# A hybrid decoder layer: block sums of the MLP weights tied to the order of ScalarE and GpSimd, a quarter of them formed in SBUF, output stores on GpSimd's queue

## The chip, the cores and the metric

One core of a Trainium2 chip runs the whole layer in one launch. The time is device microseconds (us) of the execution. Engines are TensorE (PE), VectorE (DVE), ScalarE (ACT), GpSimd (POOL) and SyncE (SP). DMAs are issued from the queues of SP, ScalarE and GpSimd, and all of them are carried out by the core's 16 DMA engines. Each engine takes its instructions in the order in which they stand.

## The reference

All in float32, 2048 tokens of width 1024, one layer:

```
h = rms_norm(x, norm1_g)
z = h @ w_in                         # 1024 x 2052, cut among four mixers: SGU (uv), S5, RG-LRU (cx, gate), attention (q, k, v, f)
y = concat(sgu(..), s5(..), rglru(..), forgetting_attention(..))
x = x + group_rms_norm(y) @ w_out
h = rms_norm(x, norm2_g)
x = x + square(relu(h @ w_mlp_in)) @ w_mlp_out      # 1024 x 4096, 4096 x 1024
return rms_norm(x, final_g)
```

## The kernel before

The layer runs in three stretches. `z_phase` multiplies the normed tokens by `w_in`, and between the matmuls emits the SGU, the RG-LRU and the set-up and scan of S5. `Att.run` does the attention, with the output projection (`wout_jobs`) filled in between; the rest of the projection follows, and stores the rows of `x1`, the input of the MLP, from GpSimd's queue (line 1369). `MLP.run` does the last two matrix products and the final norm.

Each float32 operand is split into two rounded parts: `split` makes the high part on ScalarE (line 54) and the low part on VectorE (line 58), and three matmuls stand for one product.

The MLP multiplies blocks with seven products in place of eight: tables `FIRST` and `SECOND` say for product `i` which one or two weight blocks, and which one or two token blocks, are added or subtracted first, and to which results the product goes. The tokens are worked in two halves of 1024, the 4096 inner columns in two weight halves `c`. For each pair of half and `c` there are seven groups of first products in `IN_ORDER` (1, 4, 5, 7, 3, 2, 6), and seven groups of second products in `OUT_ORDER` (3, 5, 6, 1, 2, 4, 7); a group is one `i` and 8 steps `p`, and a step is 12 matmuls. That makes 56 groups, of 96 matmuls each. Weights are made `AHEAD` = 2 steps before use.

Where product `i` needs the sum of two weight blocks, the sum is formed in DRAM ahead of time by `weight_sums`, for all such `i` but 1: a job copies 512 KB of the first block to a DRAM tile (`S1` or `S2`, line 1423, on SP's queue), and two jobs later a DMA on GpSimd's queue adds the second block to it (line 1426). There are 64 jobs: 32 for `S1` (`w_mlp_in`) and 32 for `S2` (`w_mlp_out`). `first_weight` and `second_weight` then load the finished sum with one DMA into one of five buffers of the pool `m_rw` (`weight`, line 1511). For `i` = 1 the two blocks are loaded with two DMAs into a buffer of the pool `m_raw` (line 1495), also five, which the blocks of the tokens share, and GpSimd forms the difference (`united`, line 1488).

TensorE's order is written by hand. On the other engines a scheduler places the instructions by its own estimates, within their dependences. `Clock` counts the matmul time written so far, and calls the next job of `weight_sums` at 90 and then every 8 of its units (`SUMS`). The copies wait for nothing, so that call sets no place for them on SP. What is left of the jobs after attention is written at once. The helper `behind(tc, engine)` keeps what is written inside it behind the last instruction written for that engine.

The results of the MLP are gathered in eight tiles `acc` of 128 x 1024. They are loaded from `x1` at the first step of a half (line 1654), and `finish` norms each and stores it (line 1600), both on SP's queue. The tiles of the second half are those of the first, so each load waits for the store of its tile.

Of the kernel before, what the change touches and what calls it, by code (L numbers as in the profile page):

```python
# [5 lines left out]
F32 = mybir.dt.float32  # L6
# [8 lines left out]
ADD, SUB, MUL, MAX = ALU.add, ALU.subtract, ALU.mult, ALU.max  # L15
EPS = 1e-6
SP, ACT, DVE, POOL = (getattr(mybir.EngineType, n) for n in ("SP", "Activation", "DVE", "Pool"))
# [25 lines left out]
def behind(tc, eng):  # L43

    ins = next(i for i in reversed(tc.nc.cur_bb.bb.instructions) if i.engine == eng)
    return tc.issue_after(ins)
# [1349 lines left out]
IN_ORDER = (1, 4, 5, 7, 3, 2, 6)  # L1396
OUT_ORDER = (3, 5, 6, 1, 2, 4, 7)
AHEAD = 2


def weight_sums(nc, w1, w2, S1, S2):


    jobs = []
    for c in range(2):
        def second(x):
            return w2[(c * 2 + x[0]) * 1024:(c * 2 + x[0] + 1) * 1024, x[1] * 512:(x[1] + 1) * 512]

        def first(x):
            return w1[x[1] * 512:(x[1] + 1) * 512, (c * 2 + x[0]) * 1024:(c * 2 + x[0] + 1) * 1024]  # L1410

        for S, side, table, n, at in ((S1, 0, FIRST, 128, first), (S2, 1, SECOND, 256, second)):
            for i in IN_ORDER:
                if (i, c) in S:
                    a, b, _ = table[i][side]
                    for r in range(4):
                        rs = slice(r * n, (r + 1) * n)
                        jobs.append((S[i, c][rs], at(a)[rs], at(b)[rs]))
    LAG = 2
    for n in range(len(jobs) + LAG):  # L1420
        if n < len(jobs):
            to, a, _ = jobs[n]
            nc.sync.dma_start(out=to, in_=a)
        if n >= LAG:
            to, _, b = jobs[n - LAG]
            nc.gpsimd.dma_start(out=to, in_=b, accum_op=ADD)
        yield


class MLP:  # L1430
# [80 lines left out]
        self.nc.sync.dma_start(out=flat(raw, block), in_=block)  # L1511
        return self.parts(raw)

    def weight_difference(self, blocks):
        return self.parts(self.united(self.load(blocks), -1))

    def parts(self, raw):
        wh = self.wp.tile([128, 512], F32R, tag="wh", name="wh")
# [7 lines left out]
    def first_weight(self, c, i, p):  # L1526

        a, b, sign = FIRST[i][0]
        rows = lambda w, f: w[:, f:f + 128].rearrange("(k p) f -> p k f", p=128)
        if (i, c) in self.S1:  # L1530
            return self.weight(rows(self.S1[i, c], p * 128))
        w = [rows(self.w1[x[1] * 512:(x[1] + 1) * 512], self.tile_row(c, p, x[0])) for x in (a, b) if x]
        return self.weight_difference(w) if b else self.weight(w[0])

    def second_weight(self, c, i, p):

        a, b, sign = SECOND[i][1]
        if (i, c) in self.S2:
            return self.weight(self.S2[i, c][p * 128:(p + 1) * 128])
        w = [self.w2[f:f + 128, x[1] * 512:(x[1] + 1) * 512] for x in (a, b) if x for f in (self.tile_row(c, p, x[0]),)]  # L1540
        return self.weight_difference(w) if b else self.weight(w[0])

    def hidden_side(self, i, p):

# [46 lines left out]
    def finish(self, half, tt, gf):  # L1591
        nc, sm, acc = self.nc, self.sm, self.acc[tt]
        ss = sm.tile([128, 1], F32, tag="fss", name="fss")
        rs = sm.tile([128, 1], F32, tag="frs", name="frs")
        jk = self.jkp.tile([128, self.D], BF16, tag="jk", name="jk")
        nc.scalar.activation(out=jk, in_=acc, func=AF.Square, accum_out=ss)
        rsqrt_(nc, sm, rs, ss, 1.0 / self.D, "fn")
        nc.vector.scalar_tensor_tensor(out=acc, in0=acc, scalar=rs, in1=gf, op0=MUL, op1=MUL)
        r0 = half * self.HT + tt * 128
        nc.sync.dma_start(out=self.out[r0:r0 + 128, :], in_=acc)  # L1600

    def run(self):
        nc, P, NP = self.nc, self.P, self.NP
# [45 lines left out]
        nxt, more, part = 1, iter(()), iter(())  # L1649
        for n, (half, c, out, i, p) in enumerate(steps):  # L1650
            if c == 0 and not out and i == IN_ORDER[0] and p == 0:
                for tt in range(self.HT // 128):
                    self.acc[tt] = accp.tile([128, self.D], F32, tag=f"acc{tt}", name="acc")
                    nc.sync.dma_start(out=self.acc[tt], in_=self.x1[half * self.HT // 128 + tt])
                k = self.halves.index(half) + 1
                more = self.prep(self.halves[k]) if k < len(self.halves) else iter(())
            if n % 2 and n > 10:
                next(more, None)
            make(n + AHEAD)
# [34 lines left out]


RATES = 2.3, 0.5
SUMS = 90.0, 8.0
NX, NO, XB = 2, 3, 2


def hybrid_kernel(tc, A, out, T=2048):
    nc = tc.nc
    with ExitStack() as top:
# [9 lines left out]
                 v=dp.tile([T, 4, 2, 64], F32, name="v"), ys=dp.tile([T, 1024], F32, name="ys"),  # L1713
                 negc=dp.tile([4, T], F32, name="negc"), x1=[dp.tile([128, 1024], F32, name=f"x1_{t}") for t in range(T // 128)],
                 hT=[[dp.tile([128, 512], F32, name=f"hT_{k}_{q}") for q in range(T // 512)] for k in range(8)])
        S1, S2 = ({(i, c): dp.tile(shape, F32, name=f"{nm}_{i}{c}") for i in IN_ORDER if table[i][side][1] and i != 1
                   for c in range(2)} for shape, table, side, nm in (([512, 1024], FIRST, 0, "s1"), ([1024, 512], SECOND, 1, "s2")))
        D5 = s5_scratch(dp)
        r8 = cp.tile([128, NPR], F32, name="r8")
        pool = lambda es, n, b, **k: es.enter_context(tc.tile_pool(name=n, bufs=b, reuse_waits="tile", **k))  # L1720
# [10 lines left out]
            cst["ii"] = ii  # L1731

        ck = Clock()
        sums = weight_sums(nc, A["w_mlp_in"][0], A["w_mlp_out"][0], S1, S2)
        ck.set_slow(sums, *SUMS)
        with tc.manual_schedule(engines={mybir.EngineType.PE}):
            side = ExitStack()
# [97 lines left out]
```

## Time and profile before

| | |
|---|---|
| median of 3 runs | 2598.64 us (2598.39 to 2600.78) |
| profiled execution | 2608.09 us, its span 2606.4 us |
| TensorE busy | 2211.0 us, 85% |
| VectorE busy | 1650.5 us, 63% |
| ScalarE busy | 1174.2 us, 45% |
| GpSimd busy | 749.5 us, 29% |
| mean granted TensorE clock | 0.921 of full |
| moved by DMA | 434.50 MB, mean 167 GB/s |

The profile is of one execution; busy time leaves out the issuing of DMAs. The granted clock is a share of full speed (1 is 2.4 GHz, 0.5 is 1.2 GHz). Times within the execution count from the start of its span. The stretches of the program lie about so: `z_phase` to 740 us, attention to 1210, the rest of the output projection to 1289, the MLP to 2591, and the last norms to the end.

### The profile page before, as it was taken

Reading aid. Unit: us, or ns where it says so; the run is one execution under the profiler, and the core shown is the slowest. Engines: PE = TensorE matmul, PEld = TensorE weight load, DVE = VectorE, ACT = ScalarE, POOL = GpSimd, SP = SyncE. Lnnn points to the kernel's source line nnn. Section 1 sums busy time; section 2 is a strip of 40 time slices with the busy share of each in tenths; the row PEclk is TensorE's granted clock in tenths of the full one; section 3 lists DMA queues with packets and bytes.
Section 4 is the critical chain, followed back from the end, with each engine's and each line's share of the span. In section 5 each row is a group of like instructions: output and inputs, shape, how many; then the busy total and the mean of one; then the engine's idle time right before and its main releaser. Section 6 shows DMA issues by size and latency. Waiting matters only on the chain.

```text
span 2606.4 us, 31889 instructions
## 1 busy us (share of the span) xinstructions
PE 2211.0 (85%) x10077; PEld 1796.1 (69%) x10077; DVE 1650.5 (63%) x3776; ACT 1174.2 (45%) x2351; POOL 749.5 (29%) x844
## 2 busy tenths in 40 slices
PE   6655247988957998978799999999997999999997
PEld 5443235776745787867577777888786887788886
DVE  6442234666634666744366698576986769757698
ACT  4210012543424564634257643576345763357543
POOL 2223334332220000101231374213722137232261
PEclk8777668999978999989899999999998999999999
DMA  7889988144245555537976543654437544365323
GB/s 179 241 212 270 258 191 169 59 112 144 76 134 171 172 169 186 154 110 252 325 213 198 176 152 102 191 174 144 126 120 257 174 153 129 100 196 181 97 86 113
DMA packets 338777, 434.50 MB, mean 167 GB/s; under 512 B 41840, under 2 KB 210832, under 8 KB 338352
## 3 DMA queue, kind: packets, MB, share of 16 engines
q1 hardware_dynamic: 301520, 352.63, 43.7%
q0 software_dynamic: 32704, 73.54, 11.6%
q10 hardware_dynamic: 4384, 6.29, 0.7%
q8 instruction: 80, 1.31, 0.2%
q14 instruction: 89, 0.73, 0.1%
HBM read 369.30 MB, written 130.12 MB: 192 GB/s over the span
## 4 chain that ended last, share of the span: by engine, by line
PE 47%; DMA 11%; DVE 6%; issue 3%; POOL 2%; ACT 2%; SPq 1%; ACTq 0%; POOLq 0%; DVEq 0%
PE pi L1564 7%; PE pi L1562 7%; PE pi L1563 7%; PE po L1587 6%; PE po L1588 6%; PE po L1589 6%; DMA q<-qk 3%; PE s L1087 2%; PE t L50 1%; PE po L1362 1%; DMA x<-x 1%; PE po L1364 1%; PE po L1363 1%; DMA ngc<-negc 1%; POOL s L1549 1%
## 5 line engine op out<-in xcount | busy, mean ns | idle before, releaser
L58 DVE TENSOR_TENSOR wl<-raw,wh 128x512 fp32r<-128x512 f32 x448 | 371.7, 835 | 55.9 <-ACT wh L54 54.0
L1562 PE MATMUL pi<-bh,wh 128*128 128x512 f32 x896 | 355.0, 396 | 36.2 <-ACT wh L54 26.0
L1587 PE MATMUL po<-wh,sh 128*128 128x512 f32 x896 | 353.0, 394 | 20.7 <-DVE acc L1578 17.6
L1549 POOL TENSOR_TENSOR s<-c 128x512 f32<-128x512 f32 x160 | 254.8, 1597 | 369.2 <-DVE sl L58 303.4
L1564 PE MATMUL pi<-bh,wl 128*128 128x512 f32 x896 | 353.3, 394 | 0.8 <-DVE wl L58 0.8
L1563 PE MATMUL pi<-bl,wh 128*128 128x512 f32 x896 | 352.8, 394 | 0.1
L1588 PE MATMUL po<-wl,sh 128*128 128x512 f32 x896 | 351.2, 392 | 0.0
L1488 POOL TENSOR_TENSOR raw<-raw 128x512 f32<-128x512 f32 x144 | 213.9, 1489 | 470.9 <-DMA raw<-hT 218.2
L1589 PE MATMUL po<-wh,sl 128*128 128x512 f32 x896 | 347.9, 391 | 0.0
L54 ACT CAST wh<-raw 128x512 fp32r<-128x512 f32 x448 | 276.4, 618 | 120.4 <-PE pi L1563 78.3
L1562 PEld LDWEIGHTS pi<-bh,wh 128*128 128x128 f32 x896 | 170.7, 191 | 75.0 <-ACT wh L54 27.2
L58 DVE TENSOR_TENSOR sl<-s,sh 128x512 fp32r<-128x512 f32 x160 | 189.1, 1190 | 43.6 <-ACT sh L54 40.7
L436 PE MATMUL z<-wh,hl 128*128 128x512 f32 (+1 forms) x384 | 160.4, 418 | 65.6 <-ACT wh L382 43.6
L1587 PEld LDWEIGHTS po<-wh,sh 128*128 128x128 f32 x896 | 169.6, 189 | 60.9 <-DVE acc L1578 20.4
L54 ACT CAST sh<-s 128x512 fp32r<-128x512 f32 x160 | 99.6, 622 | 246.2 <-PE po L1588 209.8
L1564 PEld LDWEIGHTS pi<-bh,wl 128*128 128x128 f32 x896 | 170.5, 190 | 39.5 <-DVE wl L58 3.8
L1563 PEld LDWEIGHTS pi<-bl,wh 128*128 128x128 f32 x896 | 170.8, 191 | 36.0 <-DVE bl L58 0.5
L1589 PEld LDWEIGHTS po<-wh,sl 128*128 128x128 f32 x896 | 169.5, 189 | 35.8
L1588 PEld LDWEIGHTS po<-wl,sh 128*128 128x128 f32 x896 | 169.8, 190 | 34.4
L438 PE MATMUL z<-wh,hl 128*128 128x512 f32 (+1 forms) x384 | 150.0, 391 | 6.9 <-DVE hl L58 6.9
L437 PE MATMUL z<-wl,hl 128*128 128x512 f32 (+1 forms) x384 | 150.6, 392 | 5.7 <-DVE wl L388 5.7
L1102 ACT ACTIVATE p<-p,ng 128x512 f32<-128x512 f32 (+3 forms) x160 | 103.8, 652 | 89.2 <-DVE ng L1098 89.1
(358 smaller groups left out, 4310.8 us busy)
## 6 DMA issues: line engine op xcount, KB each, us to landing
raw<-s SPq DMA_DIRECT2D x256, 256.0 KB
raw<-hT SPq DMA_DIRECT2D x192, 256.0 KB
raw<-in_w_mlp_in_dram SPq DMA_DIRECT2D x128, 256.0 KB
raw<-in_w_mlp_out_dram SPq DMA_DIRECT2D x128, 256.0 KB
x<-in_x_dram SPq DMA_DIRECT2D x32, 512.0 KB
s<-in_w_mlp_in_dram SPq DMA_DIRECT2D x32, 512.0 KB
s<-in_w_mlp_in_dram POOLq DMA_DIRECT2D x32, 512.0 KB, 14.2
s<-in_w_mlp_out_dram SPq DMA_DIRECT2D x32, 512.0 KB
```

The lines of the kernel that those rows point to most:

```text
L54: nc.scalar.copy(out=hi, in_=src)
L58: nc.vector.tensor_tensor(out=lo, in0=src, in1=hi.bitcast(F32), op=SUB)
L436: nc.tensor.matmul(pz, lhsT=hi[:, k, sl], rhs=wh, start=(k == 0), stop=False)
L437: nc.tensor.matmul(pz, lhsT=hi[:, k, sl], rhs=wl, start=False, stop=False)
L1488: self.nc.gpsimd.tensor_tensor(out=raw[:, 0], in0=raw[:, 0], in1=raw[:, 1], op=ADD if sign > 0 else SUB)
L1549: self.nc.gpsimd.tensor_tensor(out=s, in0=src, in1=self.C[b[1], b[0], p], op=ADD if sign > 0 else SUB)
L1562: nc.tensor.matmul(pt, lhsT=wh[:, sl], rhs=bh[:, k], start=(k == 0), stop=False)
L1563: nc.tensor.matmul(pt, lhsT=wh[:, sl], rhs=bl[:, k], start=False, stop=False)
L1564: nc.tensor.matmul(pt, lhsT=wl[:, sl], rhs=bh[:, k], start=False, stop=(k == 3))
L1587: nc.tensor.matmul(po[t], lhsT=sh[:, ts], rhs=vh, start=(p == 0), stop=False)
L1588: nc.tensor.matmul(po[t], lhsT=sh[:, ts], rhs=vl, start=False, stop=False)
L1589: nc.tensor.matmul(po[t], lhsT=sl[:, ts], rhs=vh, start=False, stop=(p == self.NP - 1))
```

## The change

The jobs of the sums are tied to the order of ScalarE and GpSimd where they are written: the copy is issued from ScalarE's queue behind ScalarE's last instruction, the add from GpSimd's queue behind GpSimd's last, three jobs later in place of two. `S1` is kept for `c` = 0 alone, so there are 48 jobs, called at 110 and then every 9 units. For `c` = 1 the first weights of `i` = 5, 7, 2 and 6 are loaded as two blocks, as those of `i` = 1 are, and united on GpSimd with the table's sign. `acc` tile `p` is loaded in step `p` of the fourth group (`i` = 7) of a half, behind SP's last instruction. The final stores go out from GpSimd's queue.

```diff
-def weight_sums(nc, w1, w2, S1, S2):
+def weight_sums(tc, w1, w2, S1, S2):
...
-    LAG = 2
+    LAG = 3
     for n in range(len(jobs) + LAG):
         if n < len(jobs):
             to, a, _ = jobs[n]
-            nc.sync.dma_start(out=to, in_=a)
+            with behind(tc, ACT):
+                nc.scalar.dma_start(out=to, in_=a)
         if n >= LAG:
             to, _, b = jobs[n - LAG]
-            nc.gpsimd.dma_start(out=to, in_=b, accum_op=ADD)
+            with behind(tc, POOL):
+                nc.gpsimd.dma_start(out=to, in_=b, accum_op=ADD)
         yield
...
-    def weight_difference(self, blocks):
-        return self.parts(self.united(self.load(blocks), -1))
+    def weight_pair(self, blocks, sign):
+        return self.parts(self.united(self.load(blocks), sign))
...
-        return self.weight_difference(w) if b else self.weight(w[0])
+        return self.weight_pair(w, sign) if b else self.weight(w[0])
...
-        nc.sync.dma_start(out=self.out[r0:r0 + 128, :], in_=acc)
+        nc.gpsimd.dma_start(out=self.out[r0:r0 + 128, :], in_=acc)
...
             if c == 0 and not out and i == IN_ORDER[0] and p == 0:
-                for tt in range(self.HT // 128):
-                    self.acc[tt] = accp.tile([128, self.D], F32, tag=f"acc{tt}", name="acc")
-                    nc.sync.dma_start(out=self.acc[tt], in_=self.x1[half * self.HT // 128 + tt])
                 k = self.halves.index(half) + 1
                 more = self.prep(self.halves[k]) if k < len(self.halves) else iter(())
+            if c == 0 and not out and i == IN_ORDER[3]:
+                self.acc[p] = accp.tile([128, self.D], F32, tag=f"acc{p}", name="acc")
+                with behind(self.tc, SP):
+                    nc.sync.dma_start(out=self.acc[p], in_=self.x1[half * self.HT // 128 + p])
...
-SUMS = 90.0, 8.0
+SUMS = 110.0, 9.0
...
-        S1, S2 = ({(i, c): dp.tile(shape, F32, name=f"{nm}_{i}{c}") for i in IN_ORDER if table[i][side][1] and i != 1
-                   for c in range(2)} for shape, table, side, nm in (([512, 1024], FIRST, 0, "s1"), ([1024, 512], SECOND, 1, "s2")))
+        S1 = {(i, 0): dp.tile([512, 1024], F32, name=f"s1_{i}0") for i in IN_ORDER if FIRST[i][0][1] and i != 1}
+        S2 = {(i, c): dp.tile([1024, 512], F32, name=f"s2_{i}{c}") for i in OUT_ORDER if SECOND[i][1][1] and i != 1 for c in range(2)}
```

The order in which the instructions stand, at three places. In these rows a tile `s_21` is the sum of product 2 for `c` = 1 (`S1` where it comes from `w_mlp_in`, `S2` where from `w_mlp_out`), and `raw` takes blocks of weights or tokens.

SP in `z_phase`, before: the last copies of the sums and the loads of `w_in` (line 377) that follow them.

```order
L711 DMA dT<-in_s_d_dram 16x8x1
L1423 DMA s_21_122<-in_w_mlp_in_dram 128x1024 x2
L1423 DMA s_61_124<-in_w_mlp_in_dram 128x1024 x4
L1423 DMA s_41_126<-in_w_mlp_out_dram 256x512 x4
L1423 DMA s_71_128<-in_w_mlp_out_dram 256x512 x4
L1423 DMA s_31_130<-in_w_mlp_out_dram 256x512 x4
L1423 DMA s_61_132<-in_w_mlp_out_dram 256x512 x2
L377 DMA raw<-in_w_in_dram 128x256 x6
```

The same place on SP now:

```order
L711 DMA dT<-in_s_d_dram 16x8x1
L377 DMA raw<-in_w_in_dram 128x256 x10
L377 DMA raw<-in_w_in_dram 128x2x256 x4
L377 DMA raw<-in_w_in_dram 128x260 x3
L406 DMA x<-in_x_dram 128x1024 x4
```

And ScalarE now, at its second copy of a sum, behind a store of the S5 input `zb` (line 565):

```order
L563 COPY zb<-z 128x256
L565 DMA zb<-zb 128x256
L1426 DMA s_50_117<-in_w_mlp_in_dram 128x1024
L382 ACTIVATE wh<-raw,g_172 128x256 x2
L561 ACTIVATE gg<-z 128x256
```

No copy of a sum is left on SP, and ScalarE has them one at a time between its own work; on SP the loads of `w_in` stand next to each other.

GpSimd at the end of attention, before: the last scaled outputs of the attention are stored to `ys`, then rows of `x1`.

```order
L1369 DMA x_14_83<-x 128x1024
L1166 TENSOR_SCALAR yo<-yo,rs 128x256 x4
L1167 DMA ys<-yo 128x4x256
L1369 DMA x_15_84<-x 128x1024
L1369 DMA x_1_70<-x 128x1024
L1369 DMA x_2_71<-x 128x1024
```

And now:

```order
L1369 DMA x_14_83<-x 128x1024
L1166 TENSOR_SCALAR yo<-yo,rs 128x256 x4
L1167 DMA ys<-yo 128x4x256
L1430 DMA s_31_122<-in_w_mlp_out_dram 256x512 x3
L1430 DMA s_61_124<-in_w_mlp_out_dram 256x512 x4
L1369 DMA x_15_84<-x 128x1024
L1369 DMA x_1_70<-x 128x1024
L1369 DMA x_2_71<-x 128x1024
```

Seven adds of sums have come between the store of `ys` and the next store of `x1` (an eighth stands a little ahead); each waits for its copy.

SP where the first half of the tokens ends and the second begins, before: final stores, loads of `acc`, and the two blocks of the first weights (line 1495).

```order
L1511 DMA raw<-in_w_mlp_in_dram 128x4x128 x3
L1600 DMA out_dram<-acc 128x1024
L1511 DMA raw<-in_w_mlp_in_dram 128x4x128
L1600 DMA out_dram<-acc 128x1024
L1654 DMA acc<-x_4_73 128x1024
L1495 DMA raw<-hT_0_105 128x512
L1654 DMA acc<-x_5_74 128x1024
L1600 DMA out_dram<-acc 128x1024 x2
L1495 DMA raw<-hT_0_89 128x512
L1654 DMA acc<-x_6_75 128x1024
L1654 DMA acc<-x_7_76 128x1024
L1495 DMA raw<-in_w_mlp_in_dram 128x4x128 x2
```

GpSimd at the same place now, with the stores among the adds of weight and token blocks (line 1492 is line 1488 of before):

```order
L1553 TENSOR_TENSOR s<-c 128x512 x10
L1604 DMA out_dram<-acc 128x1024 x3
L1492 TENSOR_TENSOR raw<-raw 128x512
L1604 DMA out_dram<-acc 128x1024
L1492 TENSOR_TENSOR raw<-raw 128x512 x3
L1604 DMA out_dram<-acc 128x1024 x2
L1492 TENSOR_TENSOR raw<-raw 128x512 x2
L1604 DMA out_dram<-acc 128x1024 x2
L1492 TENSOR_TENSOR raw<-raw 128x512 x13
```

The stores have left SP for GpSimd, and the loads of `acc` have left this place for the fourth group.

## Rows read from the trace of the kernel before

**Rows 1.** The page: the span in 40 slices, tenths (clock, load of DMA engines).

```profile
PEclk8777668999978999989899999999998999999999
DMA  7889988144245555537976543654437544365323
```

**Rows 2.** Windows by stage; the first line names the columns.

```profile
core 0: us, PE busy (x) PEld busy (x) DVE busy (x) ACT busy (x) POOL busy (x), PEclk, DMA share, GB/s
...
80.00:440.00 360.00, 185.57 (x682) 136.36 (x683) 138.24 (x767) 50.95 (x116) 118.27 (x172) 0.71 0.96 234
440.00:740.00 300.00, 274.07 (x1372) 221.93 (x1371) 198.54 (x424) 140.29 (x320) 97.03 (x202) 0.97 0.34 101
740.00:1200.00 460.00, 380.87 (x1999) 314.71 (x1997) 254.38 (x806) 219.47 (x573) 43.83 (x119) 0.91 0.50 158
1200.00:1289.30 89.30, 70.66 (x315) 55.14 (x314) 36.70 (x86) 27.95 (x55) 16.68 (x23) 0.90 0.91 312
```

**Rows 3.** TensorE's waits, 80 to 440 us: total us, times, longest us.

```profile
PE z L436 <- ACT wh L382: 43.6, 5, 35.6
PE z L448 <- ACT uvs L572: 43.4, 1, 43.4
```

**Rows 4.** ScalarE's waits, 80 to 440 us.

```profile
ACT wh L382 <- DMA raw<-in_w_in_dram: 96.2, 16, 43.9
ACT uvs L572 <- DMA ys<-uvs: 39.6, 1, 39.6
```

**Rows 5.** Timeline of SP's queue: start us, us, line, operation.

```profile
278.63 48.49 SPq L1423 DMA_DIRECT2D s<-in_w_mlp_out_dram  x14
328.77 10.38 SPq L377 DMA_DIRECT2D raw<-in_w_in_dram  x6
```

**Rows 6.** Line 1426's instructions: ns least/median/most, first and last start us.

```profile
L1426 POOL DMA_DIRECT2D s<-in_w_mlp_in_dram x32: 805/866/1619, 62.9 to 380.6; - x32
L1426 POOL DMA_DIRECT2D s<-in_w_mlp_out_dram x32: 881/1026/1634, 180.1 to 427.3; - x32
```

**Rows 7.** Windows of five groups of the MLP (columns as in rows 2).

```profile
1289.30:1323.30 34.00, 27.08 (x96) 20.68 (x97) 16.78 (x15) 16.06 (x29) 15.74 (x11) 0.82 0.97 316
...
1641.30:1663.10 21.80, 21.80 (x98) 18.04 (x97) 10.89 (x15) 12.73 (x25) 8.17 (x6) 1.00 0.64 195
1684.80:1706.60 21.80, 21.80 (x98) 18.02 (x97) 12.74 (x20) 11.63 (x20) 4.30 (x3) 1.00 0.57 181
1706.60:1728.40 21.80, 21.80 (x98) 18.06 (x97) 15.22 (x24) 18.03 (x32) 1.30 (x1) 1.00 0.51 157
1954.70:1993.70 39.00, 25.46 (x97) 19.71 (x96) 24.68 (x69) 17.65 (x34) 8.15 (x6) 0.78 0.89 297
```

**Rows 8.** Timelines of ScalarE and GpSimd, at work beside which sums now stand.

```profile
90.14 1.06 ACT L408 ACTIVATE jk<-x 128x1024 bf16<-128x1024 f32 x1 [2.35 <-DMA x<-in_x_dram]
...
244.40 0.50 ACTq L555 DMA_DIRECT2D qk<-qh  x1
...
355.04 0.41 ACTq L565 DMA_DIRECT2D zb<-zb  x1
...
439.82 0.19 POOL L500 COPY ht<-h 128x1 f32<-128x1 f32 x1 [1.39 <-DVE h L498]
```

**Rows 9.** Timeline of GpSimd, end of attention.

```profile
1210.63 0.53 POOL L1369 DMA_DIRECT2D x<-x  x1 [0.99 <-DVE x L1366]
```

**Rows 10.** Timeline of SP's queue between the halves.

```profile
1945.81 0.36 SPq L1600 DMA_DIRECT2D out_dram<-acc  x1
...
1972.75 2.87 SPq L1654 DMA_DIRECT2D acc<-x  x3
```

**Rows 11.** GpSimd's groups in the MLP: busy us, mean ns.

```profile
L1488 POOL TENSOR_TENSOR raw<-raw 128x512 f32<-128x512 f32 x139 | 207.2, 1493 | 462.5 <-DMA raw<-hT 217.4 <-ACT c L1573 56.1 <-DMA raw<-s 32.9
```

**Rows 12.** The chain that ended last: its last piece.

```profile
2601.29 1.28 DVE acc L1598
```

**Rows 13.** DMA issues of the page: last figure is us to landing.

```profile
x<-x POOLq DMA_DIRECT2D x31, 512.0 KB, 6.1
```

More of the change, by code (lines that the diff above doesn't have):

```diff
@@ L1398 @@
 AHEAD = 2
-def weight_sums(nc, w1, w2, S1, S2):
+def weight_sums(tc, w1, w2, S1, S2):
+    nc = tc.nc
     jobs = []
@@ L1540, in second_weight @@
         w = [self.w2[f:f + 128, x[1] * 512:(x[1] + 1) * 512] for x in (a, b) if x for f in (self.tile_row(c, p, x[0]),)]
-        return self.weight_difference(w) if b else self.weight(w[0])
+        return self.weight_pair(w, sign) if b else self.weight(w[0])
     def hidden_side(self, i, p):
@@ L1733, in hybrid_kernel @@
         ck = Clock()
-        sums = weight_sums(nc, A["w_mlp_in"][0], A["w_mlp_out"][0], S1, S2)
+        sums = weight_sums(tc, A["w_mlp_in"][0], A["w_mlp_out"][0], S1, S2)
         ck.set_slow(sums, *SUMS)
```

## The prediction

> **What bounds the kernel now.** The times come first: the profiled execution took 2608.1 us (span 2606.4), the median of the three runs is 2598.6, so the sum below is made against 2608.1 and 9.5 us are taken off at the end. Then the slices of the page. TensorE's granted clock and the load of the DMA engines go in opposite directions: from the second slice to the sixth (65 to 391 us) the DMA row stands at 8 or 9 tenths and the clock at 6 or 7; in the eighth to the eleventh DMA is at 1 to 4 and the clock at 9 [rows 1]. The windows by stage say how much that is. From 80 to 440 us TensorE is busy 185.6 of 360 us at a granted clock of 0.71, with the DMA engines at 0.96; in the 300 us that follow, in the same program stage, it does twice as many matmuls (1372 against 682) in 274.1 busy us at 0.97, with DMA at 0.34 [rows 2]. So the first stage waits for data.
>
> Who waits for what: TensorE lost 43.6 us to the casts of `w_in` weights and 43.4 us to a gelu of the `uv` columns [rows 3]. ScalarE, which makes both, waited 96.2 us for the loads of `w_in` and 39.6 us for a `ys` store to free its tile [rows 4]. On SP's queue, 14 of the sums' copies held the queue from 278.6 us for 48.5 us, and the next six `w_in` loads stand right behind them, at 328.8 [rows 5]. On GpSimd's queue, which also issues the `ys` stores, the 64 accumulating halves run from 62.9 to 427.3 us [rows 6]. Sums fill the saturated window. The MLP, half of the time, is different: a group of 8 steps (96 matmuls) takes 21.8 us wherever its window is full, and the excess is in few places, above all the first group of each half: 34.0 and 39.0 us [rows 7].
>
> **The change part by part.**
>
> *Copies to ScalarE's order, accumulates tied to GpSimd's, 48 jobs in place of 64.* In the order lists SP loses the block of copies that stood ahead of the `w_in` loads. On ScalarE one copy stands behind a square that the trace of before has at 90.1 us; the next stands behind a `zb` store of 355.0 us, and the rest follow one by one to the end of attention. The first accumulate stands behind a copy of GpSimd's that ran at 439.8 us [rows 8]. So 80 to 440 is freed of nearly all sums. Worth: at least the two big waits, 43.4 + 35.6 (the longest of the cast waits) = 79 us. At most: 682 matmuls at the pace of the next stage, 682 / 1372 x 300 = 149 us, saves 360 - 149 = 211. VectorE has 138 us of work in the window [rows 2], much of it dependent short setup steps, so it can't be all. I take 150: above the middle, because the smaller waits also lead back to loads and stores.
>
> *Where those 47 jobs go.* One job is a copy and an accumulate of 0.52 MB each. 64 jobs are 67 of the 84 MB of the window (234 GB/s x 360), so 0.8 x 0.96 x 360 / 64 = 4.3 us of all DMA engines per job. 47 jobs are 202 us, put into about 760 us whose load is 0.34 to 0.50 [rows 2]; the mean rises to about 0.7. Nothing in before shows this load spread out. Bounds: 0, and the price of the saturated window, 211 / 60 = 3.5 us a job, 165 in all. Since 0.7 is nearer to the stages that run at full clock, I take 25, with ScalarE's 48 issues of 0.5 us [rows 8] in it: 24 us on an engine that is busy 219 of 460 there.
>
> *The end of attention.* What the clock of the program has not issued is issued at once: four copies on ScalarE, eight accumulates on GpSimd, and behind them in GpSimd's order the stores of `x1`. There DMA is at 0.91 already [rows 2], and the first `x1` store that now stands behind them left at 1210.6 us [rows 9]; the projection's next `x` loads need the tiles that such stores free. The DMA work is 4 to 8 jobs, 17 to 34 us, of which 8 fit the gaps: 0 to 26 us, I take 15.
>
> *The `acc` loads* leave the start of each half, and the output stores leave SP. In the first group of the first half (excess 34.0 - 21.8 = 12.2 us) DMA is at 0.97 [rows 7]; 4.2 of its 10.7 MB go away: minus 8 (0 to 12.2). At the second half SP's order was stores of finished tiles, `acc` loads that wait for them, and the first weights behind: the last three loads are issued at 1972.8 us, 18 us after the group began at 1954.7 [rows 7, 10]. After, SP has only weights and tokens there. But GpSimd now has eight stores among the adds that make these weights, and each waits for VectorE's last step on its tile; the adds behind wait too. So minus 12 of the 17.2 (0 to 17.2). The loads arrive again one per step in the fourth group: 4.2 MB in 21.8 us is 193 GB/s on top of 157, 350 against 316 at a load of 0.97 [rows 7]: 2.3 us a half, plus 6 for both (0 to 24, the excess of the first group twice).
>
> *The dropped quarter.* For the second weight half (c = 1) groups 5, 7, 2 and 6 now load two blocks and add them on GpSimd: 4 x 8 x 2 = 64 adds of 1.49 us = 95 us on GpSimd [rows 11], 12 us a group of 21.8. Group 1 has such adds today: GpSimd is busy 8.2 of its 21.8 us, TensorE all of them, DMA 0.64 [rows 7]. So the adds themselves are hidden in GpSimd's idle time; if they were not, 95 us would be the price. But four such groups come nearly in a row and share five buffers with the tokens' blocks; DMA there goes from 181 to 277 GB/s. Bounds 0 and the 12.2 us of the pair group with DMA at 0.97, for eight groups 98; I take 1.75 each, plus 14.
>
> *The tail.* The last `acc` step runs from 2601.3 to 2602.6 us [rows 12], and the span ends 3.8 us later. A store of this size from GpSimd's queue takes 6.1 us to land [rows 13] and 0.53 to issue [rows 9]; SP issued in 0.36 [rows 10]: plus 0.2 to 2.5, I take 1.5. For plain transfers the Trainium skill (DMA: Bandwidth & Descriptors, SWDGE vs HWDGE vs iDMA) points to SP or ACT, and it gives the first byte as about 1 us from GpSimd against 0.6: by that estimate the tail would be longer by 0.4 us. The order of the two agrees with the issue times.
>
> Sum: -150 + 25 + 15 - 8 - 12 + 6 + 14 + 1.5 = -108.5, so 2499.6 beside the profiled 2608.1, and **2490 us** as a median.
>
> **The rivals.**
>
> *The early stage is bound by its own chain* (VectorE's setup steps and the casts), and only the two big waits go: -79 in place of -150, 2561 us. For it: VectorE's 138 us; against: the casts themselves wait for loads. If all of it came, -211, 2429 us.
>
> *The sums cost the same wherever they run.* Place: 440 to 1200 us, where scores wait for loads of q and k, and projections for tiles that queue behind sums. Price 3.5 us per job, 165 us in place of 25: 2630 us, slower than before. It decides from 25 + 108.5 = 133 us, 2.8 us a job. Against it: the load there has room, and the order places one copy at a time. The Trainium skill (DMA: Bandwidth & Descriptors, Issuing engines are not separate DMA queues) says that DMAs from all issuing engines run on the same 16 DMA engines, so that another issuer saves only issue time, usually small beside the transfer. By that rule alone the copies' move is worth nothing and the gain would be the dropped 16 jobs, 16 x 4.3 = 69 us, 2530 us. Here the issue time was not small: 48.5 us for 14 [rows 5].
>
> *The pair groups become bound by loads and their five buffers*: 98 us in place of 14, 2574 us. For it: the one pair group at a load of 0.97 lost 12.2 us. Against: that group also had the `acc` loads.
>
> **Chances.** Forecast 0.57 (its own range 2440 to 2535); only the big waits 0.21; pair groups 0.09; all of it 0.05; given back 0.08. A measurement here tells 0.2% (5 us) from no change. Faster 0.89, since all but the given-back case lie below, less a little for sums of several costs; same 0.03; slower 0.08. The range from 2430 to 2578 takes in the pair groups and the early-stage bound and leaves out most of the given-back case.
>
> **What would show it.** Windows of the first 440 us: DMA well under 0.9 until the accumulates start, clock near 0.9, the first 682 matmuls of that stretch done some 150 us earlier, no wait over 20 us for `w_in`. From there to the end of attention DMA at 0.6 to 0.8 and no longer than before by over 40 us. The first group of the second half near 27 us. Groups 5, 7, 2 and 6 of c = 1 under 25 us. Wrong would be: attention longer by over 100 us, or pair groups over 30 us.

## The result, and the profile after

The changed kernel takes 2513.32 us (median of 4 runs, 2509.57 to 2516.41) beside 2599.71 for the kernel before (4 runs, 2598.39 to 2602.62): ratio 0.9666, 95% interval 0.9647 to 0.9684. The forecast was 2490, its range 2430 to 2578. The profiled execution took 2509.57 us, the shortest of the four, and its span is 2507.9.

The slices of the page, the same two rows as [rows 1]:

```profile
PEclk8899998997789989798999999999999999999999
DMA  7535457546577776478876544874448533487323
```

The load of the DMA engines is no longer piled up in slices 2 to 6; it is spread over the first half, and the dips of the clock (7 in slices 10, 11 and 17) have moved with it.

TensorE's order is the same in both kernels, so a stretch is bounded best by the same matmuls. The windows of the changed kernel, from TensorE's 274th matmul (counted from 0, here and below) to its 956th, to its 2328th (start of attention), to its 4327th (end of attention), to the first of the MLP:

```profile
core 0: us, PE busy (x) PEld busy (x) DVE busy (x) ACT busy (x) POOL busy (x), PEclk, DMA share, GB/s
74.60:263.90 189.30, 159.55 (x684) 121.63 (x683) 132.62 (x730) 52.54 (x119) 60.10 (x112) 0.91 0.41 106
263.90:589.20 325.30, 280.91 (x1374) 224.33 (x1373) 194.76 (x419) 138.33 (x319) 112.64 (x220) 0.94 0.60 159
589.20:1104.10 514.90, 392.54 (x2001) 322.90 (x2000) 256.04 (x812) 221.38 (x578) 62.11 (x139) 0.86 0.65 185
1104.10:1210.00 105.90, 73.31 (x312) 57.70 (x310) 35.21 (x81) 26.81 (x48) 23.06 (x30) 0.82 0.95 303
```

And of the kernel before, between the same matmuls (they lie within 5 us of the bounds of [rows 2]):

```profile
81.40:440.20 358.80, 185.73 (x683) 136.43 (x684) 137.04 (x763) 51.15 (x116) 117.87 (x172) 0.71 0.96 233
440.20:740.60 300.40, 274.47 (x1373) 222.35 (x1372) 198.41 (x424) 140.09 (x320) 97.26 (x202) 0.97 0.34 102
740.60:1204.90 464.30, 382.24 (x2001) 315.34 (x2000) 256.37 (x812) 220.81 (x578) 43.59 (x119) 0.91 0.51 160
1204.90:1289.30 84.40, 68.69 (x311) 53.98 (x309) 34.64 (x80) 26.61 (x48) 16.68 (x23) 0.90 0.91 308
```

The first stretch became 169.5 us shorter (and began 6.8 us earlier), and each of the next three became longer: by 24.9, 50.6 and 21.5 us. Of 176.3 us gained by the 956th matmul, 97.0 are gone when the MLP begins, at 1210.0 in place of 1289.3.

In the early stretch one of the two waits of [rows 3] is gone, that for `uvs`; the other is 4.9 us in place of 43.6, and ScalarE's longest wait for `w_in` is 8.6 in place of 43.9 [rows 4]. TensorE's wait for `wh`, and ScalarE's two waits of [rows 4], from 80 to 264 us now:

```profile
PE z L436 <- ACT wh L382: 4.9, 3, 3.3
...
ACT wh L382 <- DMA raw<-in_w_in_dram: 39.4, 13, 8.6
...
ACT uvs L572 <- DMA ys<-uvs: 11.2, 1, 11.2
```

What took their place stands in attention. TensorE's waits there, first before (740.6 to 1204.9 us), then now (589.2 to 1104.1):

```profile
PE s L1087 <- DMA ks<-qk: 29.4, 2, 28.4
PE s L1087 <- DMA q<-qk: 17.1, 5, 4.9
PE po L1362 <- DVE x L1366: 13.9, 3, 7.7
PE s L1087 <- DVE mx L1092: 9.3, 4, 4.8
```

```profile
PE s L1087 <- DMA q<-qk: 31.8, 8, 6.0
PE s L1087 <- DMA ks<-qk: 28.7, 1, 28.7
PE s L1087 <- DVE mx L1092: 18.3, 7, 6.8
PE tp L50 <- DMA y<-ys: 17.0, 1, 17.0
PE o L1136 <- ACT ph L1123: 9.0, 1, 9.0
```

There is no single new wait. The waits for `q` grew by 14.7, one of 17.0 for `ys` is new, TensorE waits longer for VectorE's and ScalarE's softmax steps (`mx`, `ph`), and the clock fell from 0.91 to 0.86, so that the same 2001 matmuls are busy 10.3 us longer. Around the wait for `ys` SP's queue shows how the loads come late:

```profile
871.65 1.13 SPq L1041 DMA_DIRECT2D q<-qk  x2
872.82 5.14 SPq L1047 DMA_DIRECT2D ks<-qk  x1
878.40 0.40 SPq L1049 DMA_DIRECT2D ngc<-negc  x1
878.90 6.41 SPq L1348 DMA_DIRECT2D x<-x  x1
885.40 2.99 SPq L1060 DMA_DIRECT2D vs<-v  x1
888.44 8.78 SPq L1311 DMA_DIRECT2D y<-ys  x2
```

Some issues take 0.4 us here and others 3 to 8, with no copy of a sum in the queue, and SP takes its loads in order: the first of the two `y` loads is issued only when those ahead of it are. Long issues stand in the kernel before too. Summed over the trace, SP's instructions in attention took 291 us before and take 343 now.

In the MLP, four of the groups that the prediction spoke of: the first of each half (34.0 and 39.0 us before, [rows 7]) and two pair groups of c = 1 (i = 2 and 6 of the first half); a pair group is one whose weights come as two blocks that GpSimd unites:

```profile
1210.00:1234.70 24.70, 24.70 (x97) 19.80 (x98) 17.90 (x14) 15.64 (x28) 15.64 (x11) 0.89 0.96 294
...
1660.70:1683.20 22.50, 22.06 (x98) 17.95 (x97) 18.16 (x27) 14.96 (x26) 19.07 (x13) 1.00 0.84 245
1683.20:1705.70 22.50, 21.95 (x97) 17.90 (x96) 17.50 (x24) 17.05 (x31) 19.34 (x13) 1.00 0.90 285
1865.90:1893.10 27.20, 22.78 (x98) 17.80 (x97) 24.28 (x69) 17.19 (x34) 12.14 (x12) 1.00 0.82 258
```

GpSimd is busy 19 of 22.5 us in a pair group and TensorE still 22. The whole MLP, first matmul to last, went from 1301.7 to 1281.7 us.

### The profile page after: what moved, and what is told of

The parts are those of the page before. It is cut to its first block, busy times and chain, and to the rows that moved or that the text cites. A ratio compares the mean times of both kernels' runs of the same rounds, so it can differ in the third digit from the quotient of the medians.

```text
span 2507.9 us, 32062 instructions
## 1 busy us (share of the span) xinstructions
PE 2201.3 (88%) x10077; PEld 1792.2 (71%) x10077; DVE 1672.5 (67%) x3776; ACT 1169.5 (47%) x2351; POOL 832.4 (33%) x908
## 3 DMA queue, kind: packets, MB, share of 16 engines
q0 software_dynamic: 32704, 73.54, 11.9%
## 4 chain that ended last, share of the span: by engine, by line
PE 47%; DMA 15%; DVE 6%; issue 4%; POOL 3%; ACT 2%; SPq 1%; POOLq 0%; ACTq 0%; DVEq 0%
PE po L1591 6%; PE po L1592 6%; PE po L1593 6%; PE pi L1566 6%; PE pi L1567 6%; PE pi L1568 6%; DMA q<-qk 4%; DMA ngc<-negc 2%; DMA qk<-qh 2%; POOL raw L1492 2%; DMA x<-x 2%; PE t L50 1%; DMA y<-ys 1%; DMA raw<-hT 1%; PE s L1087 1%
## 5 line engine op out<-in xcount | busy, mean ns | idle before, releaser
L1492 POOL TENSOR_TENSOR raw<-raw 128x512 f32<-128x512 f32 x208 | 305.4, 1474 | 393.9 <-DMA raw<-hT 170.7
L58 DVE TENSOR_TENSOR wl<-raw,wh 128x512 fp32r<-128x512 f32 x448 | 386.2, 867 | 48.0 <-ACT wh L54 46.6
L1591 PE MATMUL po<-wh,sh 128*128 128x512 f32 x896 | 353.5, 395 | 19.9 <-DVE acc L1582 17.1
L54 ACT CAST wh<-raw 128x512 fp32r<-128x512 f32 x448 | 275.9, 616 | 103.5 <-PE pi L1567 50.9
L1591 PEld LDWEIGHTS po<-wh,sh 128*128 128x128 f32 x896 | 169.9, 190 | 59.5 <-DVE acc L1582 19.9
L436 PE MATMUL z<-wh,hl 128*128 128x512 f32 (+1 forms) x384 | 154.0, 401 | 17.3 <-ACT hl L54 9.0
L1087 PE MATMUL s<-ks,q 128*128 128x512 f32 (+3 forms) x320 | 94.4, 410 | 79.0 <-DMA q<-qk 31.8
L437 PE MATMUL z<-wl,hl 128*128 128x512 f32 (+1 forms) x384 | 144.8, 377 | 1.0 <-DVE wl L388 1.0
## 6 DMA issues: line engine op xcount, KB each, us to landing
s<-in_w_mlp_out_dram POOLq DMA_DIRECT2D x32, 512.0 KB, 11.4
```

The source lines that it names most:

```text
L54: nc.scalar.copy(out=hi, in_=src)
L58: nc.vector.tensor_tensor(out=lo, in0=src, in1=hi.bitcast(F32), op=SUB)
L436: nc.tensor.matmul(pz, lhsT=hi[:, k, sl], rhs=wh, start=(k == 0), stop=False)
L437: nc.tensor.matmul(pz, lhsT=hi[:, k, sl], rhs=wl, start=False, stop=False)
L1492: self.nc.gpsimd.tensor_tensor(out=raw[:, 0], in0=raw[:, 0], in1=raw[:, 1], op=ADD if sign > 0 else SUB)
L1591: nc.tensor.matmul(po[t], lhsT=sh[:, ts], rhs=vh, start=(p == 0), stop=False)
```

## The experiments

Each kernel was run beside the kernel before on the same chip, and the ratio is to that. The position of TensorE's 956th and 2328th matmul and the bounds of the MLP are from one profiled execution each, in us; whole runs of one kernel differ by 1 to 17 us (e5's by 20), but e1 and e2, neither of which has a job behind the 956th matmul, agree within 1 us in each stretch from there to the MLP. The number of TensorE's matmuls and their order are the same in all. e1, e6 and e9 leave the second blocks of the sums out, so their outputs are not the layer's.

| kernel | ratio, 95% interval | 956th | 2328th | MLP begins | MLP lasts |
|---|---|---|---|---|---|
| before | 1 | 440.2 | 740.6 | 1289.3 | 1301.7 |
| changed | 0.9666 (0.9647 to 0.9684) | 263.9 | 589.2 | 1210.0 | 1281.7 |
| e1 no sums | 0.9250 (0.9234 to 0.9265) | 262.3 | 556.9 | 1105.3 | 1286.4 |
| e2 untied | 0.9858 (0.9836 to 0.9881) | 416.9 | 711.5 | 1260.7 | 1287.0 |
| e3 ties alone | 0.9884 (0.9865 to 0.9904) | 270.3 | 606.1 | 1254.3 | 1308.1 |
| e4 drop alone | 0.9846 (0.9829 to 0.9863) | 397.7 | 693.4 | 1241.1 | 1307.2 |
| e5 `acc` and stores alone | 0.9940 (0.9918 to 0.9961) | 443.2 | 744.9 | 1296.0 | 1285.3 |
| e6 copies only | 0.9388 (0.9370 to 0.9406) | 263.2 | 568.3 | 1142.1 | 1284.5 |
| e7 no jobs, all pairs | 1.0353 (1.0328 to 1.0377) | 263.6 | 558.4 | 1104.2 | 1572.4 |
| e8 16 jobs | 0.9587 (0.9563 to 0.9610) | 260.2 | 576.1 | 1122.6 | 1361.1 |
| e9 small jobs | 0.9289 (0.9262 to 0.9316) | 258.5 | 555.5 | 1116.9 | 1284.7 |
| e10 32 jobs | 0.9536 (0.9508 to 0.9563) | 260.7 | 586.9 | 1165.1 | 1309.9 |
| e11 32 jobs, faster | 0.9562 (0.9535 to 0.9590) | 262.2 | 616.8 | 1163.5 | 1309.9 |
| e12 prep later | one run | 259.9 | 588.2 | 1207.3 | 1441.6 |

**What the jobs cost where they stand now: e1.**

```diff
-    for n in range(len(jobs) + LAG):
+    for n in range(0):
...
-            return self.weight(rows(self.S1[i, c], p * 128))
+            return self.weight(rows(self.w1[a[1] * 512:(a[1] + 1) * 512], self.tile_row(c, p, a[0])))
```

(and the same for `S2`).

> The changed kernel without any job of the sums: the weights that were sums in DRAM are loaded as their first block alone, by the same number of loads of the same size; the second block is left out. Load theory: the 48 jobs' transfers are what attention and the projection pay for, so this run gives back what the change lost there: TensorE's 2328th matmul (start of attention) at 565 us in place of 589, attention some 50 us shorter, the rest of the projection some 21 us shorter; total 2415 to 2435. Queue theory: only the issue time on ScalarE's and GpSimd's queues is paid, at most 48 times 0.5 us, total not under 2485. Third, the lost time has nothing to do with the sums: 2513.

The windows of e1, bounded by the same matmuls as above:

```profile
75.60:262.30 186.70, 157.75 (x684) 121.14 (x683) 133.36 (x741) 53.26 (x119) 59.54 (x111) 0.93 0.39 96
262.30:556.90 294.60, 271.44 (x1374) 220.06 (x1372) 196.62 (x419) 137.97 (x318) 95.15 (x200) 0.97 0.35 103
556.90:1019.60 462.70, 381.18 (x2001) 313.87 (x2000) 255.47 (x810) 220.46 (x578) 43.31 (x119) 0.90 0.52 159
1019.60:1105.30 85.70, 66.03 (x311) 51.92 (x310) 35.84 (x84) 26.75 (x48) 16.94 (x23) 0.89 0.89 310
```

The early stretch is as in the changed kernel, and the three behind it are back at the lengths of before, attention with 462.7 us for 464.3. So all that the changed kernel gave back is the sums' doing: 1210.0 - 1105.3 = 104.7 us for 48 jobs, 2.2 us a job. The kernel before, by the same yardstick, paid 1289.3 - 1105.3 = 184 us for 64 jobs, 2.9 each. Part of that difference is that there are fewer jobs; at equal numbers moving a job saved about 0.6 us (64 jobs: 2.9 and, in e3 below, 2.3; 48 jobs: 2.8 in e4 and 2.2).

**Bytes, or queues: e9 and e6.** In e9 the jobs are cut to a sixteenth, and the weights are read as in e1:

```diff
                         rs = slice(r * n, (r + 1) * n)
+                        rs = slice(r * n, r * n + n // 16)
```

> The changed kernel with all 48 copies and 48 adds in their places on ScalarE's and GpSimd's queues, but each of a sixteenth of its rows (32 KB); the weights are the first blocks, as in e1, and the second blocks are left out. Load theory: a sixteenth of the bytes costs nearly nothing, so the MLP begins at 1108 to 1120 us as in e1, ratio 0.925 to 0.930. Queue theory: the issues and the adds' waits for their copies stay, so at least 60 of e1's 104 us stay, ratio 0.95 or more.

The MLP begins at 1116.9, 11.6 us after e1: 96 issues and all their waits cost 11.6 of the 104.7 us, and the bytes the other 93. Attention, with every issue in its place:

```profile
555.50:1029.50 474.00, 379.71 (x2001) 312.37 (x2000) 255.44 (x810) 220.98 (x578) 60.53 (x139) 0.91 0.52 158
```

That is 11.3 us longer than in e1. So of the 52 us that the jobs cost in attention a fifth is the issues and their order, and with it a part of the waits that looked new there: in e9 TensorE still waits 10.9 us for `ys` and 15.9 for `mx`.

In e6 the copies stay whole and the adds go:

```diff
         if n >= LAG:
             to, _, b = jobs[n - LAG]
-            with behind(tc, POOL):
-                nc.gpsimd.dma_start(out=to, in_=b, accum_op=ADD)
+            pass
```

> The changed kernel without the adds: the 48 copies stay where they are, and the second blocks are left out of the sums. Load theory: the cost ahead of the MLP, 104 us of e1 against the changed kernel, follows the time that the jobs hold the DMA engines; the copies are about 1.6 of 4.3 us of a job, so about 40 us remain: MLP begins near 1150 us, ratio 0.94. ScalarE theory: the copies' issues and their place in ScalarE's order cost, so 80 us or more remain, ratio 0.955 or more. GpSimd theory: the adds that wait for copies hold back the stores behind them, so under 20 us remain, ratio under 0.933.

36.8 us remain (1142.1 - 1105.3), as the load theory had it: the copies are 0.8 us a job, and the adds, of as many bytes written and put on top of the copies, 1.4.

**Which part of the change gave what: e2 to e5.** e2 takes the ties away, and leaves the queues:

```diff
-            with behind(tc, ACT):
-                nc.scalar.dma_start(out=to, in_=a)
+            nc.scalar.dma_start(out=to, in_=a)
...
-            with behind(tc, POOL):
-                nc.gpsimd.dma_start(out=to, in_=b, accum_op=ADD)
+            nc.gpsimd.dma_start(out=to, in_=b, accum_op=ADD)
```

> The changed kernel without the ties: copies still on ScalarE's queue, adds still on GpSimd's, 48 jobs, but nothing holds them behind the last instruction written, and all copies stand among ScalarE's first 130 instructions. If the order is what gives, the load comes back into the first 440 us, DMA there at 0.9 or more, and 48 jobs cost what 64 did in proportion: early stage longer by 100 to 130 us, attention shorter by about 50, total 2560 to 2600. If taking the copies off SP's queue is what gives, the early stage stays short (TensorE's 956th matmul before 300 us) and the total is 2513 or less.

The load is back in the early stage, though no copy is on SP; the 956th matmul comes at 416.9, and the 274th, at 122.5, was late already (74.6 in the changed kernel). From the one to the other:

```profile
122.50:416.90 294.40, 170.34 (x682) 128.90 (x683) 140.59 (x784) 53.14 (x119) 92.05 (x147) 0.77 0.79 186
```

The issues of the `w_mlp_out` copies on ScalarE's queue, in e2 and then in the changed kernel (ns least/median/most, first and last start us):

```profile
L1425 ACTq DMA_DIRECT2D s<-in_w_mlp_out_dram x32: 497/765/12016, 137.2 to 273.5; - x32
L1426 ACTq DMA_DIRECT2D s<-in_w_mlp_out_dram x32: 497/498/8528, 433.6 to 1104.4; - x32
```

Summed, the 48 copies take ScalarE 85.0 us to issue in e2 and 33.2 in the changed kernel; in e4 (below), where they stand on SP without a tie, they take SP 84.9. So long issues like those of [rows 5] (41.8 of the 48.5 us there are issues, the rest gaps between them) go with copies that stand close together under load, in whichever queue they are. In e2 they hold ScalarE, which makes the casts and the gelus, while no load of `w_in` on SP takes over 0.7 us to issue between 149 and 182 us. e2 shows that another queue without the order does not free the early stage; it does not tell how much of the early stage's loss is the load of the DMA engines and how much the engine that the copies hold.

The Trainium skill (DMA: Bandwidth & Descriptors, Issuing engines are not separate DMA queues) says that another issuing engine brings no engines of its own for the transfer. e2 agrees: 0.9858 with the copies on ScalarE's queue, no better than e4's 0.9846 with them on SP's (e2 has the moved `acc` loads besides, which e4 lacks).

e3 is the kernel before with the ties and queues alone, all 64 jobs:

```diff
-            nc.sync.dma_start(out=to, in_=a)
+            with behind(tc, ACT):
+                nc.scalar.dma_start(out=to, in_=a)
...
+            with behind(tc, POOL):
...
-SUMS = 90.0, 8.0
+SUMS = 110.0, 7.0
```

> The kernel before with the ties and queues of the change alone: all 64 jobs kept, called every 7 units in place of 9 so that as many are left at the end; acc loads and final stores as before. Order theory: the early stage is freed as in the changed kernel (956th matmul at 264 us, 176 earlier than before), and later stages give back 64/48 of 96 us, 130: total 2545 to 2565. Dropping theory: the gain of the change is in its 16 dropped jobs, so this run stays at 2590 to 2610.

The early stage is freed nearly as in the changed kernel, 169.9 us by the 956th matmul, and 134.9 of them are given back by the start of the MLP: 64 jobs still cost 149 us against e1, 2.3 each. The ties alone are worth 1.2%, a little less than expected, between the totals of the two theories and near the first.

e4 is the kernel before with the dropped quarter alone:

```diff
-        S1, S2 = ({(i, c): dp.tile(shape, F32, name=f"{nm}_{i}{c}") for i in IN_ORDER if table[i][side][1] and i != 1
-                   for c in range(2)} for shape, table, side, nm in (([512, 1024], FIRST, 0, "s1"), ([1024, 512], SECOND, 1, "s2")))
+        S1 = {(i, 0): dp.tile([512, 1024], F32, name=f"s1_{i}0") for i in IN_ORDER if FIRST[i][0][1] and i != 1}
+        S2 = {(i, c): dp.tile([1024, 512], F32, name=f"s2_{i}{c}") for i in OUT_ORDER if SECOND[i][1][1] and i != 1 for c in range(2)}
```

> The kernel before with the dropped quarter alone: 48 jobs, copies on SP's queue where the scheduler puts them, the first weights of c=1 as two blocks united on GpSimd. If the early stage is bound by DMA load alone, 16 jobs of 4.3 us come off it: total 2525 to 2550. If it is bound by when SP's queue reaches the loads of w_in, the load that goes is behind those and the total is 2575 to 2600.

Between the two, about 2560 beside 2600: the MLP begins 48.2 us earlier, 3.0 a job, and lasts 5.5 longer. This part alone gives 1.5%, more than the ties.

e5 is the kernel before with the moved `acc` loads and the final stores on GpSimd's queue, as in the diff of the change.

> The kernel before with the acc loads in the fourth group and the final stores on GpSimd's queue, and nothing else. If these moves are what shortened the first groups of the two halves in the changed kernel, this run has 34.0 down to 25 and 39.0 down to 27 us there, the rest unchanged: ratio 0.992, 20 us. If the first group of the first half was shortened by the sums' going elsewhere, only the second half's 12 us come: ratio 0.995.

The first groups are 24.6 and 27.3 us in place of 34.0 and 39.0; the fourth of the first half is 26.0 in place of 25.0. The MLP is 16.4 us shorter, the ratio 0.994. So both first groups were shortened by this edit, and not by the sums' going elsewhere.

The three parts add up: 1.16 + 1.54 + 0.60 = 3.3%, and the change as a whole gave 3.34.

**Can the rest of the jobs go: e7, e8, e10, e11.** e7 empties both tables (`S1 = {}`, `S2 = {}`); the computation is full.

> The changed kernel with no sum in DRAM at all: every pair of weight blocks is loaded as two blocks and united on GpSimd, as for c=1 in the changed kernel; the full computation. The front as in e1 (MLP begins at 1108 us). 24 more groups become pair groups. If they are hidden as the eight of the changed kernel were (0 to 1 us each), the total is 2411 to 2435, ratio 0.925 to 0.934. If GpSimd becomes the bound where a group has adds for both sides (16 adds of 1.47 us in 21.8) and DMA where the first half's groups are already longer, 3 to 8 us a group: 2450 or more, ratio 0.94 or more.

Much slower, and in the main by neither of the two reasons. The MLP is 291 us longer than in the changed kernel, and 218 of them are in four groups. These, i = 5, 7, 2 and 6 of the first half's c = 0, take 78.9, 79.6, 83.5 and 79.5 us. Group 5 there, and below it the same product for c = 1, where the pair is hidden:

```profile
1154.50:1233.40 78.90, 37.65 (x101) 25.85 (x101) 14.35 (x22) 12.84 (x23) 15.20 (x12) 0.68 0.28 83
1726.40:1748.20 21.80, 21.80 (x98) 18.04 (x97) 17.60 (x20) 11.73 (x20) 14.49 (x11) 1.00 1.02 284
```

Twelve GpSimd adds and 28% of the DMA engines: nothing is busy. SP's timeline in group 7 shows one pair of loads at a time, every 7 us or so, each about as long after the last as GpSimd's wait for a pair and its add (in group 5, 44.3 us of waits in 8, and 1.3 each):

```profile
1240.67 0.93 SPq L1499 DMA_DIRECT2D raw<-in_w_mlp_in_dram  x2
1241.65 0.50 SPq L1661 DMA_DIRECT2D acc<-x  x1
1247.36 0.92 SPq L1499 DMA_DIRECT2D raw<-in_w_mlp_in_dram  x2
1253.37 0.34 SPq L1486 DMA_DIRECT2D hT<-ht  x1
1255.17 0.82 SPq L1499 DMA_DIRECT2D raw<-hT  x2
```

In these groups `prep` makes the next half's tokens: it takes four tiles of the pool `raw` (line 1469) and keeps them for most of 14 calls, one every second step, twice. Of five buffers one is left for the pairs. e12 moves `prep`:

```diff
-            if n % 2 and n > 10:
+            if n % 2 and n > 102:
```

> The changed kernel with the next half's norm and transposes (prep) begun at step 103 in place of 11, so that they fall on the first products of c=1, of which 1, 5, 7 and 2 load pairs. If prep's hold on four of the five buffers of m_raw is what made e7's pair groups of c=0 take 79 us, these groups now take about 79 us each in the first half and the groups of c=0 fall to 22: total near 2513 + 4 x 57 - 25 = 2715. If it was the traffic of c=0's place in the program, they stay under 30 us and the total is 2490 to 2520.

The slow groups moved with it. The profiled execution took 2666.85 us; the pair groups 1, 5, 7 and 2 of c = 1 now take 69.2, 60.7, 80.1 and 59.8 us, 183 above 21.8 each where 228 were expected, and the first half's groups of c = 0 behind the first fell to 21.8. Group 5 of c = 0 and group 7 of c = 1:

```profile
1253.10:1274.90 21.80, 21.80 (x97) 18.03 (x97) 12.83 (x20) 11.63 (x20) 3.69 (x3) 1.00 0.88 295
1677.60:1757.70 80.10, 37.88 (x100) 27.26 (x101) 17.31 (x26) 19.53 (x35) 13.92 (x11) 0.66 0.29 86
```

That it is `prep` is shown; that it is the buffers follows from the code and the single pairs in SP's queue. A pool with more buffers wasn't tried.

e8 keeps only the 16 jobs of `S1` (`S2 = {}`).

> The changed kernel with only the 16 jobs of w_mlp_in for c=0 kept; all sums of w_mlp_out are formed in SBUF. If a tied job costs 2.2 us ahead of the MLP (104 over 48), the MLP begins at about 1143 us; if the first 16 jobs fall where there is room (between 264 and 589 us the changed kernel lost 25 to 32 us), at about 1135. Second products with pairs add 0 to 1 us each, 16 groups. Total 2445 to 2465, ratio 0.938 to 0.945; slower than e7 unless the pair groups of c=0 of the first half cost more than 35 us there.

16 jobs early in the program cost 17.3 us (1122.6 - 1105.3), 1.1 each, less than in any other run. But the MLP lasts 79.4 us longer than in the changed kernel. The largest piece is group 6 of the first half's first products, 35.0 us for 23.5. Groups 1 of the second products, where the weights and the hidden side both need adds and group 6 ahead does too, take 26.6 to 28.1 us in place of 21.8, and the first groups of c = 1, behind group 7, 28.3 and 28.5. It is still faster than the changed kernel by its ratio.

e10 therefore keeps 6 and 7 in DRAM and forms 3 and 4 in SBUF:

```diff
-        S2 = {(i, c): dp.tile([1024, 512], F32, name=f"s2_{i}{c}") for i in OUT_ORDER if SECOND[i][1][1] and i != 1 for c in range(2)}
+        S2 = {(i, c): dp.tile([1024, 512], F32, name=f"s2_{i}{c}") for i in OUT_ORDER if SECOND[i][1][1] and i in (6, 7) for c in range(2)}
```

> The changed kernel with 32 jobs: the sums of w_mlp_out for products 3 and 4 are formed in SBUF too, where GpSimd has no or eight other adds in the group; those of 6 and 7 stay in DRAM. By the prices of e1, e3 and the changed kernel, a tied job costs 1.3 us while z_phase still runs, 2.6 in attention and 3.3 behind it: 24 jobs of 1.3 and 8 of 2.6 are 52 us, so the MLP begins near 1160; e8's groups 3 and 4 of the second products were longer by 0 to 2 us, 4 in all: total 2465, ratio 0.948. Rival: the pair groups spoil the MLP as in e8, where it took 79 us more; if they were 3 and 4, the total is over 2500, ratio 0.96.

The front came near the estimate (1165.1 for 1160); the MLP is 28 us longer than in the changed kernel in place of 4. The largest piece is group 6 of the first half again, at the end of `prep`, 34.5 us for 23.5; the first weights of the pair group behind it are made there, which fits e7 but was not tried apart. Groups 7 take 24.7 to 26.2 in three cases of four. At 0.9536 it beats both kernels: 1.3% below the changed kernel, and their intervals are apart.

e11 is e10 with `SUMS = 110.0, 6.0`.

> As e10, but a job every 6 units in place of 9, so that all are issued before attention, near 500 us. If the price goes by the stage, 32 jobs of 1.3 us are 42 and the total is 10 us under e10. If it rises with the load that is there already (0.6 between 264 and 589 us now, near 0.75 then), the two are equal within 5 us; if it goes by the load alone as in the kernel before, 2.9 us a job, e11 is 40 us slower.

The MLP begins at 1163.5, 1.6 us from e10, and the ratios overlap. Attention starts 29.9 us later than in e10 and is 32.3 shorter, with no job left in it. So there is no cheap stretch, and the price by stage with which e10 was estimated is wrong. From the 956th matmul to the 2328th, 20 copies and 20 adds cost 31.6 us against e1 in e10 (1.6 a job), and 26 copies and 30 adds 60.0 in e11 (2.1): there a job costs more where more of them stand. In attention that is not seen: e10's 8 copies and 11 adds cost 29.1 us, the changed kernel's 23 and 20 cost 52.2.

## Why the prediction was right, and where it was off

The direction and the mechanism of the gain held, and the time lies in the range, 23 us above the forecast. Term by term, against the profiled executions:

| term | predicted | measured |
|---|---|---|
| early stage freed | -150 | -176.3 |
| 47 jobs into 440 to 1200 us | +25 | +75.5 (24.9 and 50.6) |
| end of attention | +15 | +21.5 |
| first group of first half | -8 | -9.3 |
| first group of second half | -12 | -11.9 |
| `acc` loads in the fourth groups | +6 | -1.3 |
| pair groups of c = 1 | +14 | +3.0 |
| tail | +1.5 | +0.9 |
| sum | -108.5 | -97.9; the spans differ by -98.5 |

(The pair groups' +3.0 is what the eight took over 21.76 us each; the fourth group went from 25.0 to 23.7 in the first half and stayed at 21.8 in the second. The prediction's working for that term, 2.3 us a half, gives 4.6, not 6.)

The sum is closer than its terms: two came out 57 us worse than predicted and five 46.5 better, and that these errors cancel was luck. Of the 23 us, 10 are in the spans. The other 13 are the step from profile to median: the prediction took 9.5 us off, since the profiled execution of before was slower than the median, and the profiled execution of the changed kernel was 3.8 faster than its median.

**The early stage.** Every sign that the prediction named was there: DMA at 0.41, the clock at 0.91, no wait for `w_in` over 8.6 us. The gain was larger than 150, nearer to the upper bound. The reason given with it, that copies hold SP's queue ahead of the `w_in` loads, is not the whole of it: e2 has no copy on SP, and its 956th matmul is 19 us later than in e4, which has 48 there. In e2 the copies hold ScalarE instead; no run cuts the bytes of copies that stand early, so how much is the load and how much the held engine stays open.

**The term that was mis-sized: "Where those 47 jobs go".** It took 25 us between bounds of 0 and 165, "since 0.7 is nearer to the stages that run at full clock". The mean load did come to 0.60 and 0.65, as forecast, and the cost was 75.5 us, with 43 copies and 40 adds in the two stretches. A mean load under 1 was taken for room. e1 shows that the cost is all the sums', and e9 that all but 11.6 of the 104.7 us is bytes and not issues. TensorE's longer waits for `q` (31.8 us for 17.1), SP's longer issues in attention (343 us for 291) and the clock (0.86 for 0.91) show where it lands; how one load is held up by one job was not followed. Its mark of no more than 40 us longer to the end of attention was passed by 35.5; the one for wrong (100 us) was not reached.

**The rivals.** *The sums cost the same wherever they run* was nearer to the truth than its chance of 0.08 says: 2.2 us a job where they stand now, against 2.9 before. It did not decide, because the 75.5 us for the 47 jobs stayed under 133. By the rule of the Trainium skill weighed with it (DMA: Bandwidth & Descriptors, Issuing engines are not separate DMA queues), the 16 dropped jobs alone would give 69 us and 2530; e4 measures 1.5%, 40 us, for them. The result lies between that and the forecast, and e3 to e5 say why: ties, drop and `acc` each give a part, and the drop gives the most. The prediction entered it as a cost of 14 us, and at its price for a moved job (25 / 47 = 0.5 us) 16 jobs fewer were worth only 8.

*The pair groups become bound by their five buffers* did not come for c = 1, where GpSimd's adds were hidden at +3.0 us in all. e7 shows that case for c = 0: with `prep` in the pool a pair group takes 79 us. *The early stage is bound by its own chain* fell with the -176.

**`acc` and tail.** The first groups were sized well, and e5 confirms them by themselves: 16.4 us of the MLP. The tail grew by 0.9 us for 1.5.

## What to carry to other kernels

Transfers that are moved out of a saturated stretch are not free where the load is at 0.35 to 0.5: here a moved job still cost about four fifths of its price, so dropping a quarter of the transfers gave more than finding all of them a better place. A run with the transfers cut to a sixteenth, issues left in place, tells bytes from queues in one go. Before a precomputed operand is formed on the fly, look who else holds the buffers in that stretch, not only at the adds and the load.

## What the runs showed that was not expected

By these traces an add into DRAM holds the DMA engines for about twice as long as a copy of the same size. In attention of the changed kernel ScalarE's queue (q10, nearly all copies) and GpSimd's (q0) moved:

```profile
q0 software_dynamic: 10654, 23.93, 20.1%
q10 hardware_dynamic: 5990, 11.59, 7.4%
```

Before, GpSimd's queue had there:

```profile
q0 software_dynamic: 5307, 13.10, 8.0%
```

The columns are packets, MB and the share of 16 engines. Copies: 7.4% of 514.9 us for 11.59 MB, 3.3 us per MB. Adds: 103.5 us less 37.1 before (8.0% of 464.3) for 10.83 MB more, 6.1 us per MB, an estimate, since the other transfers of that queue are taken to cost the same in both. The times ahead of the MLP are in the same proportion, 0.8 and 1.4 us a job (e6).

And a stretch slows at a mean DMA load well under 1: in attention a load of 0.65 for 0.52 goes with 52 us more (the changed kernel against e1), 11.4 of them in TensorE's busy time, at a granted clock of 0.86 for 0.90, and 41 in its waits. In e9, with the issues but hardly the bytes, the load is 0.52 and 11.3 us of the 52 are there.
